# Summing squares over features: pairs of feature tiles added on GpSimd and VectorE ahead of one group of matmuls

## The chip, the cores and the metric

The kernel runs on one core of one Trainium2 chip. Its engines work side by side, each on its own queue in order: TensorE (matmul; PE in the profile, PEld for its weight loads), VectorE (DVE), ScalarE (ACT), GpSimd (POOL) and SyncE (SP, which issues most DMAs). The metric is the device time of one execution in microseconds. Before the change the median of three runs is 1806.03 us (1805.53 to 1806.41).

## What is computed

Two layers of a diffusion backbone run over 512 latent tokens and 256 context tokens, each a vector of 1024 features. What matters here is the sandwich norm around every mixer and every FFN:

```
def rms_norm(x, g):
    y = xf * lax.rsqrt(jnp.mean(xf * xf, axis=-1, keepdims=True) + EPS)
    return (y * g.astype(jnp.float32)).astype(x.dtype)

def modulate(h, shift, scale):
    return h * (1 + scale) + shift
```

A mixer or FFN gives y. The kernel computes x = x + gate * rms_norm(y), and then the next input h = modulate(rms_norm(x), shift, scale). So each token needs two sums of squares over its 1024 features: one of y, and one of the new x. Layer 0 mixes by neighbourhood attention and an mLSTM and carries both kinds of tokens; layer 1 mixes by latent attention and gives out latent tokens only. All arithmetic is float32, the large products as three products of split operands (hi and lo).

## The kernel before

Activations lie with features on the 128 partitions: eight feature tiles (KD = 8), each 128 features by a run of tokens. A run ("segment", class `Seg`) is all 512 latent tokens (`SX`), the 256 context tokens (`SC`), or one half of the latent tokens (`SH[0]`, `SH[1]`, 256 each).

The sum of squares over features runs across partitions, so TensorE makes it. `sums4` (line 390) takes four tiles of squares and multiplies each by a 128x32 matrix of ones; the four matmuls go to four column groups of the array (`tile_position`) and add into four bands of 32 partitions of one PSUM tile `ps`. Two calls, `first` and `last`, accumulate eight feature tiles. The matmul of the last tile is issued first and the other three are held behind it (`issue_after`). `sums_bc` (line 400) then copies the PSUM tile to a row (`scratch("srow")`), adds the four bands by small matmuls (`psc`), computes the inverse root (`rstd_of`: VectorE, one power instruction on GpSimd, three on VectorE) and broadcasts it over partitions by a transpose into PSUM (`bc`).

There are two places with such sums:

- `YNorm.put(m, src)` (line 420) is called once for each output tile m of an output projection or of the last down-projection group of an FFN. It squares the tile on ScalarE (`ysq`) and, after m = 3 and m = 7, calls `sums4` into `ysum`. (A 512-wide segment has another way: it adds its squares up on GpSimd in one tile, and is not touched.) The squares stand in two-tile buffers of the tag `sq`; there are two of these. The tag `sc` of `scratch` has two buffers of 128x512 as well.
- `YNorm.chain` (line 438) is a generator. Its first step makes the broadcast of y's norm; then for each k it scales y(k) on VectorE (line 453), adds it to x(k) on VectorE or, for the k of `RVO` = (1, 3) or `RVF` = (0, 2, 4), on GpSimd (line 454), squares x(k) into y(k) on ScalarE, and after k = 3 and k = 7 calls `sums4` into `pss`; then come the steps that make the modulated h. `RawNorm.chain` (line 482), for the last FFN part of layer 0, makes h from x(k) at once (lines 493 and 494) and applies the second norm later as a factor.

Chains are put in a list, and `step(n)` advances the oldest one by n steps while the next segment's projection is being traced: `out_proj` (line 1186) after each output tile, `ffn` (line 1219) in `front` and in `down`. So the chain of one segment runs beside the `put`s of the next one. Segments go in this order: out_proj of layer 0: SX, SC; FFN of layer 0: SH[1], SH[0], SC; out_proj of layer 1: SH[0], SH[1]; FFN of layer 1: SH[0], SH[1]. Of the nine `put` sequences eight use `sums4`; seven of the chains have a second norm. That makes 15 sums of 8 tiles, 30 calls of `sums4`.

The order of instructions on each engine isn't written by hand. The tile framework lays it from the order of tracing, priorities (`tc.high_priority` for weight loads) and its own idea of when operands are ready; waits and buffer releases are added by it.

The helpers in which the profile records the operations: `mm` L142, `tr` L145, `act` L148, `tt` L151, `ts` L154, `stt` L157, the matmul of `sums4` L393.

Of the kernel before, what the change touches and what calls it, by code (L numbers as in the profile page):

```python
# [9 lines left out]
F32 = mybir.dt.float32  # L10
F32R = mybir.dt.float32r
BF16 = mybir.dt.bfloat16
AF = mybir.ActivationFunctionType
ALU = mybir.AluOpType
# [3 lines left out]
KD = D // 128  # L18
# [46 lines left out]
def hybrid_backbone_kernel(ctx: ExitStack, tc: tile.TileContext, *aps):  # L65
    nc = tc.nc
    V, S, G, PE = nc.vector, nc.scalar, nc.gpsimd, nc.tensor
# [39 lines left out]
    def ps_c(name):  # L107
        if psum["split"]:
            psum["j"] = psum.get("j", 0) + 1
            return ps_t("yx"[psum["j"] % 2], name)  # L110
        return ps_t("c" if "c" in psum["n"] else "w", name)
# [26 lines left out]
    def instr(i):  # L138
        return getattr(i, "ins", i)

    def mm(o, l, r, start, stop):
        return PE.matmul(out=o, lhsT=l, rhs=r, start=start, stop=stop)  # L142
# [4 lines left out]
    def act(o, i, func=AF.Copy, **kw):  # L147
        S.activation(out=o, in_=i, func=func, **kw)  # L148

    def tt(e, o, x, y, op):  # L150
        e.tensor_tensor(out=o, in0=x, in1=y, op=op)  # L151

    def ts(e, o, x, s1, s2, op0, op1):
        e.tensor_scalar(out=o, in0=x, scalar1=s1, scalar2=s2, op0=op0, op1=op1)  # L154

    def stt(o, x, s, y, op0, op1):
        V.scalar_tensor_tensor(out=o, in0=x, scalar=s, in1=y, op0=op0, op1=op1)  # L157
# [6 lines left out]
    def fr(ap):  # L164
        return ap.bitcast(F32)
# [187 lines left out]
    sqp = ctx.enter_context(tc.tile_pool(name="sqp", bufs=2, reuse_waits="tile"))  # L353

    def scratch(name):
        return sqp.tile([128, 512], F32, tag="sc", name=name, bufs=2)

    def rstd_bc(pss, n, dim, name):

        return bcasts(rstd_of(pss[:, :n], n, dim), n, name)  # L360
# [29 lines left out]
    def sums4(ps, w, srcs, first, last):  # L390

        def one(i):
            return PE.matmul(out=ps[32 * i:32 * i + 32, 0:w], lhsT=ones32, rhs=srcs[i], start=first, stop=last,  # L393
                             tile_position=(0, 32 * i))
        n_ = len(srcs) - 1
        with tc.issue_after(instr(one(n_))):
            for i in range(n_):
                one(i)

    def sums_bc(ps, sg, name):  # L400

        row = scratch("srow")
        act(row[:, 0:sg.w], ps[:, 0:sg.w])
        psc = ps_c("psc")
        for j in range(sg.nt):
            mm(psc[:, j:j + 1], row[:, j * 128:(j + 1) * 128], sel4[:, 0:1], True, True)
        return rstd_bc(psc, sg.nt, D, name)

    class YNorm:


# [8 lines left out]
        def put(self, m, src):  # L420
            w = self.sg.w
            if self.wide:
                if m == 0:
                    act(self.acc, src, AF.Square)
                else:
                    sq = scratch("ysq")
                    act(sq[:, :w], src, AF.Square)
                    tt(G, self.acc, self.acc, sq[:, :w], ALU.add)
                return
            if m % 2 == 0:  # L430
                self.t = sqp.tile([128, 512], F32, tag="sq", name="ysq")
            sq = self.t[:, 256 * (m % 2):256 * (m % 2) + w]
            act(sq, src, AF.Square)
            self.sq.append(sq)
            if m % 4 == 3:
                sums4(self.ps, w, self.sq[-4:], m == 3, m == KD - 1)

        def chain(self, x, y, Gt, mod=None, done=None):


            sg = self.sg
            w, c = sg.w, sg.mc
            if self.wide:
                pss = ps_c("pssy")
                for j in range(sg.nt):
                    mm(pss[:, j:j + 1], self.acc[:, j * 128:(j + 1) * 128], ones_c, True, True)
                bc = rstd_bc(pss, sg.nt, D, "y")
            else:
                bc = sums_bc(self.ps, sg, "y")
            yield  # L450
            ps2 = ps_c("pss") if mod else None
            for k in range(KD):
                stt(y(k), y(k), Gt[:, k, c:c + 1], bc[:, :w], ALU.mult, ALU.mult)
                tt(G if k in (RVF if done and mod else RVO) else V, x(k), y(k), x(k), ALU.add)
                if mod:
                    act(y(k), x(k), AF.Square)
                    if k % 4 == 3:
                        sums4(ps2, w, [y(k - 3 + i) for i in range(4)], k == 3, k == KD - 1)
                else:
                    done(k)  # L460
                yield
            if mod:
                bc = sums_bc(ps2, sg, "m")
                yield
                A, B, h = mod
                for k in range(KD):
                    hi, lo = (t[:, k, sg.ho:sg.ho + w] for t in h)
                    b = B[:, k, c:c + 1]
                    stt(y(k), x(k), A[:, k, c:c + 1], bc[:, :w], ALU.mult, ALU.mult)
                    if k in (LGF if done else LGO):  # L470
                        ts(G, y(k), y(k), 1.0, b, ALU.mult, ALU.add)
                        act(hi, y(k))
                        tt(G, lo, y(k), fr(hi), ALU.subtract)
                    else:
                        act(hi, y(k), AF.Identity, bias=b)
                        stt(lo, y(k), b, fr(hi), ALU.add, ALU.subtract)
                    yield

    class RawNorm(YNorm):


        def chain(self, x, y, Gt, mod, done):
            sg = self.sg
            w, c = sg.w, sg.mc
            A, h = mod
            bc = sums_bc(self.ps, sg, "y")
            yield
            self.ps2 = ps_c("pss")
            for k in range(KD):
                stt(y(k), y(k), Gt[:, k, c:c + 1], bc[:, :w], ALU.mult, ALU.mult)  # L490
                tt(G if k in RVF else V, x(k), y(k), x(k), ALU.add)
                hi, lo = (t[:, k, sg.ho:sg.ho + w] for t in h)
                act(hi, x(k), AF.Copy, scale=A[:, k, c:c + 1])
                stt(lo, x(k), A[:, k, c:c + 1], fr(hi), ALU.mult, ALU.subtract)
                act(y(k), x(k), AF.Square)
                if k % 4 == 3:
                    sums4(self.ps2, w, [y(k - 3 + i) for i in range(4)], k == 3, k == KD - 1)
                yield

        def factor(self, y):  # L500
# [10 lines left out]
    with ExitStack() as l0:  # L511
# [20 lines left out]
        for k in range(KD):  # L532
            sq = x0p.tile([128, T], F32, tag="sq0", name="sq0", bufs=4)
# [168 lines left out]
        for i in range(7):  # L702
            src, dst = runs[i % 2], runs[1 - i % 2]
# [1093 lines left out]
```

## Time and profile before

| | |
|---|---|
| median of 3 runs | 1806.03 us |
| the profiled execution | 1806.48 us |
| its span, first to last instruction | 1804.3 us |
| mean granted TensorE clock | 0.991 |
| TensorE busy | 1739.2 us (96%), 10498 matmuls |
| VectorE busy | 1163.0 us (64%), 2210 instructions |
| ScalarE busy | 748.2 us (41%), 1297 |
| GpSimd busy | 253.7 us (14%), 306 |

The profile is of one execution. A row of the page gives an engine's busy time, its share of the span and its instructions. A row of a group names line, engine, operation, the tiles written and read, the shape, the count, then busy time and the mean in ns, then the idle time of the engine ahead of these instructions and what ended it. A row of a timeline gives start and duration in us from the span's start, and in square brackets the idle time just ahead with its releaser. `x8` means that eight records were merged into a row. A matmul's recorded duration overlaps the next one's, so the distance of starts tells what it costs. The tile name `acc` stands for y (line 1194 and line 1316), so a square of the new x in a chain is a ScalarE row `acc<-x`; `ysq` is a square in `put`, `ysum` and `pss` are the PSUM tiles of the two kinds of sums.

### The profile page before, as it was taken

The numbers are of one execution on the slowest core, as the hardware profiler recorded it, in microseconds if no ns is written. First come the engines' busy times: TensorE is split into PE (matmuls) and PEld (weight loads), VectorE is DVE, ScalarE is ACT, GpSimd is POOL, SyncE is SP. The second block draws the span as 40 slices with busy tenths as digits, with TensorE's granted clock in tenths as the row PEclk, the third lists the DMA queues.
The fourth block names the chain that finished last, engine by engine and source line by source line (L and its number), as shares of the span: only waits on it lengthen the run. The fifth ranks groups of instructions, "written<-read, shape, count | busy, mean of one in ns | idle before, by whom it ended". The sixth has DMA issues, their size and how long they took to land.

```text
span 1804.3 us, 26608 instructions
## 1 busy us (share of the span) xinstructions
PE 1739.2 (96%) x10498; PEld 1454.0 (81%) x10498; DVE 1163.0 (64%) x2210; ACT 748.2 (41%) x1297; POOL 253.7 (14%) x306
## 2 busy tenths in 40 slices
PE   6999999999999999999999999899999999999997
PEld 4777887887878888888888888788878888888885
DVE  3384577558266686676764657788894574556555
ACT  3333344444344422132221335577784454333242
POOL 1000024224320000000000002444451200000001
PEclk8999999999999999999999999999999999999998
DMA  9343332113312343444322211000012132224231
GB/s 307 106 139 129 95 112 88 53 54 127 96 36 94 120 130 108 137 127 132 120 87 70 82 47 48 24 12 13 13 36 85 50 115 87 89 86 135 72 94 47
DMA packets 63260, 162.39 MB, mean 90 GB/s; under 512 B 6272, under 2 KB 19792, under 8 KB 63136
## 3 DMA queue, kind: packets, MB, share of 16 engines
q1 hardware_dynamic: 61616, 156.52, 27.6%
q0 software_dynamic: 1376, 4.04, 0.7%
q8 instruction: 83, 1.36, 0.3%
q14 instruction: 41, 0.34, 0.1%
q10 hardware_dynamic: 144, 0.13, 0.0%
HBM read 158.57 MB, written 2.10 MB: 89 GB/s over the span
## 4 chain that ended last, share of the span: by engine, by line
PE 83%; DVE 7%; POOL 3%; issue 2%; DMA 2%; ACT 2%; DVEq 0%; POOLq 0%; ACTq 0%
PE pu L142 29%; PE pd L142 14%; PE sp L142 4%; PE qkp L142 3%; PE yps L142 3%; PE puf L142 3%; PE vtk L142 3%; PE pdl L142 3%; PE qp L142 2%; PE ot L142 2%; PE pt L145 2%; PE vp L142 2%; PE kp L142 2%; DMA aw<-in_ada_w_dram 1%; DVE acc L157 1%
## 5 line engine op out<-in xcount | busy, mean ns | idle before, releaser
L148 ACT ACTIVATE whi<-wraw 128x1024 fp32r<-128x1024 f32 x186 | 195.4, 1058 | 478.8 <-PE pu L142 221.1
L151 DVE TENSOR_TENSOR wlo<-wraw,whi 128x1024 fp32r<-128x1024 f32 x184 | 224.9, 1227 | 236.1 <-ACT whi L148 235.4
L142 PE MATMUL pu<-h,whi 128*128 128x258 f32 (+1 forms) x1280 | 318.5, 339 | 0.0
L142 PEld LDWEIGHTS pu<-h,whi 128*128 128x128 f32 x1280 | 219.6, 188 | 28.7 <-issue 0.8
L142 PE MATMUL pd<-hid,whi 128*128 128x512 f32 (+1 forms) x864 | 233.4, 358 | 1.5 <-DVE acc L151 1.5
L142 PE MATMUL pu<-h,wlo 128*128 128x512 f32 (+1 forms) x640 | 216.6, 339 | 0.0
L142 PEld LDWEIGHTS pd<-hid,whi 128*128 128x128 f32 x864 | 152.2, 188 | 28.6 <-DVE acc L151 3.1
L151 POOL TENSOR_TENSOR ry<-rv,mhalf 128x2 f32<-128x2 f32 (+2 forms) x26 | 24.1, 928 | 999.2 <-DVE rv L154 997.8
L142 PE MATMUL pd<-hid,wlo 128*128 128x512 f32 (+1 forms) x432 | 153.1, 356 | 0.0
L151 DVE TENSOR_TENSOR acc<-pd,acc 128x512 f32<-128x512 f32 (+1 forms) x192 | 109.2, 586 | 50.0 <-PE pd L142 48.7
L142 PEld LDWEIGHTS pu<-h,wlo 128*128 128x128 f32 x640 | 120.9, 189 | 13.7
L142 PE MATMUL pu<-hb,whi 128*128 128x512 f32 x304 | 119.5, 393 | 0.0
L142 PE MATMUL pu<-hb,wlo 128*128 128x512 f32 x304 | 119.3, 392 | 0.0
L142 PE MATMUL pu<-lb,whi 128*128 128x512 f32 x304 | 118.2, 389 | 0.0
L157 DVE SCALAR_TENSOR_TENSOR av<-aw,s,av 128x512 f32<-128x512 f32 x140 | 102.5, 749 | 18.9 <-DMA aw<-in_ada_w_dram 18.2
L154 POOL TENSOR_SCALAR P<-P,rl 128x768 f32<-128x768 f32 (+1 forms) x96 | 85.1, 889 | 140.4 <-DVE nm L154 49.1
L142 PEld LDWEIGHTS pd<-hid,wlo 128*128 128x128 f32 x432 | 81.2, 188 | 11.9
L157 DVE SCALAR_TENSOR_TENSOR u<-pu,c_ffn_conv,u 128x769 f32<-128x769 f32 x80 | 81.1, 1014 | 10.4 <-ACT u L148 9.7
L142 PE MATMUL sp<-kr,qh 128*128 128x512 f32 (+1 forms) x256 | 71.0, 353 | 2.5 <-ACT P L148 1.3
L151 DVE TENSOR_TENSOR pTl<-pt,pTh 128x512 fp32r<-128x512 f32 x96 | 64.5, 682 | 5.6 <-ACT pTh L148 4.8
L142 PEld LDWEIGHTS pu<-hb,wlo 128*128 128x128 f32 x304 | 57.1, 188 | 13.1
L142 PEld LDWEIGHTS pu<-lb,whi 128*128 128x128 f32 x304 | 57.1, 188 | 12.8
(454 smaller groups left out, 3799.9 us busy)
## 6 DMA issues: line engine op xcount, KB each, us to landing
wraw<-in_ffn_up_dram SPq DMA_DIRECT2D x88, 512.0 KB, 3.6
aw<-in_ada_w_dram SPq DMA_DIRECT2D x112, 256.0 KB, 2.8
wraw<-in_ffn_down_dram SPq DMA_DIRECT2D x44, 512.0 KB, 3.6
aw<-in_ada_w_dram SPq DMA_DIRECT2D x40, 512.0 KB, 4.6
wraw<-in_w_in_dram SPq DMA_DIRECT2D x20, 512.0 KB, 3.5
wraw<-in_w_tok_dram SPq DMA_DIRECT2D x8, 512.0 KB, 4.3
wraw<-in_w_out_dram SPq DMA_DIRECT2D x8, 512.0 KB, 3.6
wraw<-in_w_o_dram SPq DMA_DIRECT2D x8, 512.0 KB, 3.5
```

The lines of the kernel that those rows point to most:

```text
L142: return PE.matmul(out=o, lhsT=l, rhs=r, start=start, stop=stop)
L145: PE.transpose(out=o, in_=i, identity=ident[0:i.shape[0], 0:i.shape[0]])
L148: S.activation(out=o, in_=i, func=func, **kw)
L151: e.tensor_tensor(out=o, in0=x, in1=y, op=op)
L154: e.tensor_scalar(out=o, in0=x, scalar1=s1, scalar2=s2, op0=op0, op1=op1)
L157: V.scalar_tensor_tensor(out=o, in0=x, scalar=s, in1=y, op0=op0, op1=op1)
```

## The change

Squares of tiles k and k + 4 are added to each other before TensorE sums them. A new helper `pair` adds the square of tile k into the one of tile k - 4, in place: on GpSimd for k = 4, 5 and 6, on VectorE for k = 7. `sums4` is then called once for each run, with four tiles, first and last at once, after k = 7. In `put` the first four squares keep the two buffers of the tag `sq`, and the last four go to `scratch` tiles (`ysq2`). In both chains y(k) is added into y(k - 4). The wide way of `put` and the first norm of the kernel (line 536) are as they were.

```diff
+    def pair(sq, sq2, k):
+
+        tt(V if k == KD - 1 else G, sq, sq, sq2, ALU.add)
+
     class YNorm:
...
-            if m % 2 == 0:
-                self.t = sqp.tile([128, 512], F32, tag="sq", name="ysq")
-            sq = self.t[:, 256 * (m % 2):256 * (m % 2) + w]
-            act(sq, src, AF.Square)
-            self.sq.append(sq)
-            if m % 4 == 3:
-                sums4(self.ps, w, self.sq[-4:], m == 3, m == KD - 1)
+            if m < 4:
+                if m % 2 == 0:
+                    self.t = sqp.tile([128, 512], F32, tag="sq", name="ysq")
+                self.sq.append(self.t[:, 256 * (m % 2):256 * (m % 2) + w])
+                act(self.sq[m], src, AF.Square)
+            else:
+                if m % 2 == 0:
+                    self.t = scratch("ysq2")
+                sq = self.t[:, 256 * (m % 2):256 * (m % 2) + w]
+                act(sq, src, AF.Square)
+                pair(self.sq[m - 4], sq, m)
+            if m == KD - 1:
+                sums4(self.ps, w, self.sq, True, True)
...
                     act(y(k), x(k), AF.Square)
-                    if k % 4 == 3:
-                        sums4(ps2, w, [y(k - 3 + i) for i in range(4)], k == 3, k == KD - 1)
+                    if k >= 4:
+                        pair(y(k - 4), y(k), k)
+                    if k == KD - 1:
+                        sums4(ps2, w, [y(i) for i in range(4)], True, True)
...
                 act(y(k), x(k), AF.Square)
-                if k % 4 == 3:
-                    sums4(self.ps2, w, [y(k - 3 + i) for i in range(4)], k == 3, k == KD - 1)
+                if k >= 4:
+                    pair(y(k - 4), y(k), k)
+                if k == KD - 1:
+                    sums4(self.ps2, w, [y(i) for i in range(4)], True, True)
```

## The prediction

> **What bounds the kernel now.** I began with the page: the span, the busy times, and the chain that ended last.
>
> ```profile
> span 1804.3 us, 26608 instructions
> PE 1739.2 (96%) x10498; PEld 1454.0 (81%) x10498; DVE 1163.0 (64%) x2210; ACT 748.2 (41%) x1297; POOL 253.7 (14%) x306
> PE 83%; DVE 7%; POOL 3%; issue 2%; DMA 2%; ACT 2%; DVEq 0%; POOLq 0%; ACTq 0%
> ```
>
> TensorE is busy for 96% of the span and is 83% of the chain, so a matmul taken away is worth its time wherever TensorE has other work ready. GpSimd has 86% of the span free and VectorE 36%, but those are averages: the edit lies in four short stretches (about 450 to 540, 1060 to 1130, 1370 to 1430 and 1766 to 1793 us), and what counts is who is late there.
>
> Next I asked for the line of the summing matmuls (L393), on TensorE alone. The last two rows are TensorE's idle time ahead of them, with its releaser and the number of waits.
>
> ```profile
> L393 PE MATMUL ysum<-ysq,ones x128: 379/391/403, 499.0 to 1792.0; 128*32 128x256 f32 x128
> L393 PE MATMUL pss<-acc,ones x112: 379/403/617, 496.8 to 1428.6; 128*32 128x256 f32 x96, 128*32 128x512 f32 x16
>   ACT acc L148: 3.8, 5
>   ACT ysq L148: 2.8, 3
> ```
>
> There are 240 records. A group is four matmuls, and each float32 matmul leaves two records (a group shows as x8 below), so there are 30 groups: two for each of 15 runs of tokens, eight in `put` (ysum) and seven in the chains (pss). One pss run is 512 wide, all others 256. Half the groups go: 120 records.
>
> **What a group costs TensorE.** The third view is TensorE's timeline at the first two groups (start, duration).
>
> ```profile
> 496.39 0.28 PE L142 MATMUL yps<-h,wlo 128*128 128x256 f32 x1
> 496.51 0.28 PE L142 MATMUL yps<-h,whi 128*128 128x256 f32 x1
> 496.77 1.07 PE L393 MATMUL pss<-acc,ones 128*32 128x512 f32 x8
> 497.76 0.38 PE L142 MATMUL yps<-h,whi 128*128 128x256 f32 x1
> 497.99 0.28 PE L142 MATMUL yps<-h,wlo 128*128 128x256 f32 x1
> ...
> 498.69 0.28 PE L142 MATMUL yps<-h,wlo 128*128 128x256 f32 x1
> 498.81 0.28 PE L142 MATMUL yps<-h,whi 128*128 128x256 f32 x1
> 499.02 0.64 PE L393 MATMUL ysum<-ysq,ones 128*32 128x256 f32 x8
> 499.59 0.39 PE L142 MATMUL yps<-h,whi 128*128 128x256 f32 x1
> 499.81 0.29 PE L142 MATMUL yps<-h,wlo 128*128 128x256 f32 x1
> ```
>
> Ends overlap, so starts are what to read. Ordinary 256-wide matmuls start 0.12 us apart. Into the 256-wide group it is 0.21, from its start to the next matmul 0.57, and to the one after that 0.22: a group costs 0.09 + 0.57 + 0.10 = 0.76 us. The 512-wide one costs 0.14 + 0.99 + 0.11 = 1.24. Term one: 14 x 0.76 + 1.24 = 11.9 us less TensorE work.
>
> **What is added.** Each run gets three adds on GpSimd and one on VectorE: 45 and 15. These rows are groups of instructions: the nearest GpSimd adds (whole trace), and VectorE's in the last 50 us.
>
> ```profile
> L151 POOL TENSOR_TENSOR x<-acc,x 128x256 f32<-128x256 f32 x14 | 11.8, 840 | 21.2 <-DVE acc L157 21.2
> L151 POOL TENSOR_TENSOR ysq<-ysq 128x512 f32<-128x512 f32 x7 | 9.1, 1302 | 23.2 <-ACT ysq L148 23.2
> L151 DVE TENSOR_TENSOR x<-acc,x 128x256 f32<-128x256 f32 x12 | 4.8, 423 | 0.0
> ```
>
> So 0.84 us (512 wide: 1.30) per GpSimd add and 0.42 per VectorE add. [...]
>
> Together the GpSimd adds are about 39 us on an engine that is 14% busy. What counts is not their sum but when the last of them is done, for now one group waits for all eight squares, and whatever stands behind it on TensorE waits too.
>
> **The added step in `put`.** There the eight squares are paced by TensorE, one per output tile of about 1.4 us, so adds 4, 5 and 6 are done before square 7. Add 7 on VectorE comes between the last square and the group: 0.42 plus a hand-off of 0.04, 0.46 us. In six of the eight puts the next tile's or the next stage's matmuls are ready and can be laid ahead of the group; I cost these at nothing, and if that cover is missing it is 0.46 each, 2.8 in all. Two puts wait for their last square already, and there the step is exposed: 517.17 and the end of the kernel, 0.92 together. At the end the order is matmul, VectorE add, square, group, as these rows from the timelines show, among them groups I need below.
>
> ```profile
> 517.17 0.64 PE L393 MATMUL ysum<-ysq,ones 128*32 128x256 f32 x8 [1.06 <-ACT ysq L148]
> ...
> 1081.57 0.64 PE L393 MATMUL pss<-acc,ones 128*32 128x256 f32 x8 [0.68 <-ACT acc L148]
> ...
> 1086.62 0.40 ACT L148 ACTIVATE acc<-x 128x256 f32<-128x256 f32 x1
> 1086.75 0.48 DVE L157 SCALAR_TENSOR_TENSOR h<-x,A,h 128x256 fp32r<-128x256 f32 x1
> 1087.63 0.64 PE L393 MATMUL pss<-acc,ones 128*32 128x256 f32 x8
> ...
> 1790.81 0.42 DVE L151 TENSOR_TENSOR acc<-pdl,acc 128x256 f32<-128x256 f32 x1 [1.00 <-PE pdl L142]
> 1791.27 0.42 ACT L148 ACTIVATE ysq<-acc 128x256 f32<-128x256 f32 x1 [0.95 <-DVE acc L151]
> 1791.74 0.64 PE L393 MATMUL ysum<-ysq,ones 128*32 128x256 f32 x8 [0.97 <-ACT ysq L148]
> ```
>
> **The seven chains.** Here the squares hang on VectorE, not on TensorE. When the first group goes, so does its wait: of the 6.6 us of waits above, 1.06 and 0.97 are at last groups of puts, so 4.6 are at first groups. That isn't a gain by itself: TensorE reaches the one group earlier and waits there. Take the pair 1081.57 and 1087.63. Without the first group and its wait TensorE stands at the second at 1087.63 - 0.76 - 0.68 = 1086.19. Square 7 ends at 1087.02; VectorE is in another instruction until about 1087.2, adds, and hands over at about 1087.67. The wait is 1.48 where 0.68 was: +0.80. I take +0.80 for five of the 256-wide chains, 4.0 us. The sixth (chain of the context tokens in layer 0) gets 0: its last two squares, the first of the next rows, end at 527.18, and its second group starts seven microseconds later; other matmuls fill the time.
>
> ```profile
> 526.43 0.75 ACT L148 ACTIVATE acc<-x1c 128x256 f32<-128x256 f32 x2 [0.64 <-DVE x1c L151]
> ...
> 534.21 0.64 PE L393 MATMUL pss<-acc,ones 128*32 128x256 f32 x8
> ```
>
> The 512-wide chain is worse. Its squares and VectorE's residual adds:
>
> ```profile
> 496.08 1.67 ACT L148 ACTIVATE acc<-x 128x512 f32<-128x512 f32 x3
> 498.85 1.15 ACT L148 ACTIVATE acc<-x 128x512 f32<-128x512 f32 x2
> ...
> 497.42 1.29 DVE L151 TENSOR_TENSOR x<-acc,x 128x512 f32<-128x512 f32 x2
> ...
> 501.82 1.07 PE L393 MATMUL pss<-acc,ones 128*32 128x512 f32 x8
> ```
>
> And this is how a GpSimd add meets a VectorE instruction that reads two SBUF tensors:
>
> ```profile
> 1077.46 0.74 POOL L151 TENSOR_TENSOR x<-acc,x 128x256 f32<-128x256 f32 x1 [0.37 <-DVE acc L157]
> 1077.66 0.82 DVE L157 SCALAR_TENSOR_TENSOR h<-x,A,h 128x256 fp32r<-128x256 f32 x1 [0.28 <-ACT h L148]
> ...
> 1079.86 0.47 DVE L157 SCALAR_TENSOR_TENSOR h<-x,A,h 128x256 fp32r<-128x256 f32 x1
> ```
>
> The same instruction takes 0.47 us alone and 0.82 beside GpSimd, ending 0.28 after it: VectorE stood still for 0.35. So in the 512-wide chain add 4 (from 497.3 to 498.6) holds the sixth residual add up; they then take turns, VectorE to 499.25, GpSimd (add 5) to 500.55, VectorE to 501.2, GpSimd (add 6) to 502.5, VectorE (add 7) to 503.2. TensorE would stand there at 501.82 - 1.24 = 500.58 and wait 2.7 us. [...]
>
> Sum: -11.9 + 0.9 (two puts) + 4.0 (five chains) + 2.7 (the wide chain) = **-4.3 us**. Bounds: the last add could cost nothing anywhere (-11.9, and no better, since the first groups' waits are waits for the same squares), or 0.46 in the six covered puts too (-1.5).
>
> Nothing else is on the path. ACT issues the same squares, and no DMA moves. The two scratch buffers now also hold squares 4 to 7 of a `put` and are shared with the row copies of the sums; those come behind the last square. The squares 0 to 3 hold both buffers of their tag to the end of the put, where the next put wanted them anyway. VectorE's add 7 waits for ACT; behind it stand residual adds and PSUM additions of the next tile, which TensorE needs to get its PSUM banks back. Behind the adds that wait on GpSimd stand its residual adds and the power step of the next norm; since GpSimd is free for most of each stretch, I cost that at nothing, and if it is wrong at one add, 0.84, for the norm that it holds up.
>
> **Own time and median.** The profiled execution took 1806.48 us, 2.2 more than its span; the median of the runs is 1806.03. I take the sum off the median: 1806.0 - 4.3 = 1801.7 us.
>
> **Rivals.**
>
> (a) The order of instructions on each engine isn't written in the kernel; it will be laid anew, and if other matmuls fill every wait in the chains, only the two exposed puts pay: -11.9 + 0.9 = -11.0, 1795.0. For it: after most groups the next instruction is an unrelated matmul. Against: the five waits for ACT acc above, 3.8 us in all, show that the order fits the real squares only to about 0.8 us.
>
> (b) The gain is eaten. Each chain's three GpSimd adds hold VectorE up by 0.35 each, 1.05 per chain, in five chains 5.3 us if all hit and 2.6 if half do. -4.3 + 2.6 to -4.3 + 5.3 is -1.7 to +1.0: 1804.3 to 1807.0, no difference.
>
> (c) Slower: VectorE becomes the bound in the last down-projection of the first FFN. The view by stretches there:
>
> ```profile
> 1075.00:1088.00 13.00, 11.42 (x100) 9.64 (x100) 11.56 (x29) 8.37 (x22) 2.21 (x3) 1.00 0.00 0
> 1094.00:1107.00 13.00, 12.02 (x104) 10.05 (x103) 11.78 (x29) 9.49 (x24) 3.40 (x5) 1.00 0.02 4
> ```
>
> Columns after the length are TensorE, its weight loads, VectorE, ScalarE and GpSimd busy. VectorE has 1.2 to 1.4 us free of 13. In each stretch a chain and the next put run together: six GpSimd adds, 6 x 0.35 = 2.1, and add 7, 0.42, are 2.5 us. It decides from the point where more than half of the six hit a two-input instruction. Then on top of (b)'s 5.3 come the puts' adds, 2 x 1.05 here and 1.05 in the output projection of layer 1, and two adds 7 (0.84): -4.3 + 5.3 + 3.2 + 0.8 = +5.0, 1811.0. [...] Against it: about half of VectorE's instructions there read PSUM (the scaling by the broadcast, the additions of products) and run beside GpSimd, and between the stretches VectorE has room.
>
> That the change does nothing of what it says can be excluded: fewer matmuls are issued.
>
> **How the numbers follow.** About 0.2%, 3.6 us, is what a measurement of this kernel can tell from no change. Forecast 0.33, (a) 0.17, (b) 0.30, (c) 0.20. The forecast's middle is just over the line, so I count 0.02 of it as no difference: faster 0.48, same 0.32, slower 0.20. For the range I leave out the far half of (a) and most of (c): 1796.5 to 1809.5. Within faster and same alone it would be 1796.5 to 1807.
>
> **What would show it.** Right: 10378 matmuls on TensorE, 120 records at L393; TensorE's busy time 9 to 11 us lower; eight ysum and seven pss groups, with the pss groups waiting 1 to 3 us each and for an add on GpSimd or VectorE, no longer for ACT; 0.46 more at the end between the last square and the group. (a) would show TensorE's waits at L393 under 3 us in all. (b) and (c) would show two-input instructions of VectorE at 0.8 where they took 0.42 to 0.47, and (c) both stretches longer than 13 us. Wrong would be a gain or loss that comes from stages without these sums: then the new order of the instructions, not the sums, has decided.

## The result and the profile after

The change makes the kernel slower: 1824.55 us (median of 5 runs, 1823.20 to 1825.62) against 1806.23 us before on the same chip (1805.53 to 1806.93), a ratio of 1.0104 (95% interval 1.0091 to 1.0117). The forecast was 1801.7, the range ended at 1809.5. The profiled execution took 1825.62 us, its span is 19.4 us longer than before. Of all executions in this document one, of `e12` below, ran at a granted clock of 0.842 and took 1925.00 us; it is left out of the figures. The page after:

```profile
span 1823.7 us, 26435 instructions
PE 1743.6 (96%) x10378; PEld 1459.2 (80%) x10378; DVE 1174.1 (64%) x2225; ACT 748.3 (41%) x1297; POOL 297.6 (16%) x351
```

The 120 records are gone as said, yet TensorE is busy 4.4 us longer, not 9 to 11 us shorter: some of its work ran slower. With 19.4 us more span and 4.4 more busy it also stood still 15 us more. The view of TensorE's waits says for what (engine, tile, line, releaser; us in total, times, longest):

```profile
PE pdl L142 <- DVE acc L151: 8.2, 11, 2.2
PE ysum L393 <- DVE ysq L151: 6.2, 3, 4.5
PE puf L142 <- ACT whi L148: 2.6, 1, 2.6
PE pss L393 <- DVE acc L151: 1.2, 2, 1.1
PE pss L393 <- POOL acc L151: 0.8, 3, 0.4
```

At the groups themselves (the rows with L393) it is 8.2 us, against 6.6 before: the waits that the prediction had thought about hardly grew in sum, though one of them, 4.5 us, is new. The row at the top is another thing: products of the down-projection (`pdl`) that wait until VectorE has emptied their PSUM bank. Before it was

```profile
PE pdl L142 <- DVE acc L151: 1.7, 4, 0.6
```

Where the time went is read by stages. I cut each trace at the same three pairs of matmuls: the output projection of layer 0, the first FFN's last down-projection with what overlaps it, and the output projection of layer 1. The view by stretches of the kernel before (window, length, then busy us of TensorE, its weight loads, VectorE, ScalarE, GpSimd, the granted clock, DMA share, GB/s):

```profile
486.65:563.27 76.62, 73.14 (x492) 61.72 (x492) 54.30 (x103) 38.55 (x75) 16.70 (x16) 1.00 0.16 49
1039.85:1170.86 131.01, 119.79 (x890) 103.98 (x888) 91.26 (x222) 63.80 (x139) 30.98 (x37) 0.99 0.13 40
1364.10:1473.81 109.71, 104.61 (x778) 93.22 (x777) 64.34 (x117) 55.28 (x106) 15.67 (x17) 1.00 0.25 78
```

and of the kernel after:

```profile
488.09:573.47 85.38, 77.34 (x481) 64.54 (x481) 62.87 (x116) 39.76 (x78) 30.41 (x25) 0.96 0.18 56
1049.29:1187.48 138.19, 118.39 (x842) 103.18 (x841) 96.29 (x228) 64.06 (x139) 44.69 (x55) 0.99 0.12 38
1380.60:1493.63 113.03, 107.07 (x746) 96.58 (x745) 66.93 (x121) 55.58 (x106) 27.17 (x29) 0.95 0.25 75
```

The three stages grew by 8.8, 7.2 and 3.3 us, together 19.3 of the 19.4. Three different things are to be seen. In the first and third the granted clock fell: the trace's clock record has TensorE at half rate (a granted clock of 0.50) for 6.8 and 10.2 us there, where before had none, which costs half of it by estimate, 3.4 and 5.1. In the middle stage the clock is as before (3.4 us at half in both), TensorE's busy time fell by 1.4, and it stands still 19.8 us (138.19 - 118.39) instead of 11.2, while VectorE is busy 5.0 longer. And by the same estimate the third stage without its clock loss would have *gained* 1.8 us.

### The profile page after: what moved, and what is told of

The parts are those of the page before. It is cut to its first block, busy times and chain, and to the rows that moved or that the text cites. A ratio compares the mean times of both kernels' runs of the same rounds, so it can differ in the third digit from the quotient of the medians.

```text
span 1823.7 us, 26435 instructions
## 1 busy us (share of the span) xinstructions
PE 1743.6 (96%) x10378; PEld 1459.2 (80%) x10378; DVE 1174.1 (64%) x2225; ACT 748.3 (41%) x1297; POOL 297.6 (16%) x351
## 4 chain that ended last, share of the span: by engine, by line
PE 80%; DVE 9%; POOL 3%; ACT 2%; DMA 2%; issue 2%; DVEq 0%; ACTq 0%; POOLq 0%
PE pu L142 29%; PE pd L142 13%; PE puf L142 4%; PE sp L142 4%; PE qkp L142 3%; PE vtk L142 3%; PE yps L142 3%; PE qp L142 2%; PE pt L145 2%; PE ot L142 2%; PE vp L142 2%; PE kp L142 2%; PE pdl L142 2%; DVE wlo L151 1%; DVE acc L157 1%
## 5 line engine op out<-in xcount | busy, mean ns | idle before, releaser
L151 POOL TENSOR_TENSOR ysq<-ysq,ysq 128x256 f32<-128x256 f32 x24 | 19.7, 823 | 878.9 <-ACT ysq L148 878.9
L142 PEld LDWEIGHTS pd<-hid,wlo 128*128 128x128 f32 x432 | 81.2, 188 | 11.9
L142 PE MATMUL pdl<-hid,whi 128*128 128x256 f32 x320 | 61.1, 289 | 8.4 <-DVE acc L151 8.2
```

## The first stage in close-up

The 512-wide chain, on the timelines of GpSimd, VectorE and TensorE (the first row is three adds, the second is the first of them alone):

```profile
498.82 7.76 POOL L151 TENSOR_TENSOR acc<-acc 128x512 f32<-128x512 f32 x3 [2.55 <-ACT acc L148]
498.82 5.32 POOL L151 TENSOR_TENSOR acc<-acc 128x512 f32<-128x512 f32 x1 [2.55 <-ACT acc L148]
...
498.87 1.28 DVE L151 TENSOR_TENSOR x<-acc,x 128x512 f32<-128x512 f32 x2
500.07 1.22 DVE L151 TENSOR_TENSOR wlo<-wraw,whi 128x1024 fp32r<-128x1024 f32 x1
501.20 0.68 DVE L151 TENSOR_TENSOR acc<-acc 128x512 f32<-128x512 f32 x1
501.81 1.22 DVE L151 TENSOR_TENSOR wlo<-wraw,whi 128x1024 fp32r<-128x1024 f32 x1
...
502.71 1.04 PE L393 MATMUL pss<-acc,ones 128*32 128x512 f32 x2
504.19 1.04 PE L393 MATMUL pss<-acc,ones 128*32 128x512 f32 x2 [0.44 <-POOL acc L151]
505.41 1.04 PE L393 MATMUL pss<-acc,ones 128*32 128x512 f32 x2 [0.17 <-POOL acc L151]
506.63 1.05 PE L393 MATMUL pss<-acc,ones 128*32 128x512 f32 x2 [0.17 <-POOL acc L151]
507.61 0.51 PE L142 MATMUL yps<-h,whi 128*128 128x256 f32 x2
```

The first GpSimd add takes 5.32 us, the other two about 1.25 each. The prediction had the two engines take turns. Here they did not: VectorE goes through five instructions with two SBUF inputs without a pause, until 503.02, each at its usual length, and the GpSimd add ends 1.12 us after that. Two of the five are splits of weights, which stand at this place before the change too and which the prediction had not put into its turns. The four matmuls of the group, which before ran side by side in four column groups and took 0.99 us from their start to the next matmul, now start one by one as their squares arrive: 4.90 us from the first to the next matmul, most of it shown as *busy*. Then the `put` of the context tokens:

```profile
517.83 0.28 PE L142 MATMUL yps<-h,wlo 128*128 128x256 f32 x1
517.91 2.26 DVE L157 SCALAR_TENSOR_TENSOR h<-acc,mod,h 128x512 fp32r<-128x512 f32 x2
518.29 1.04 ACT L148 ACTIVATE whi<-wraw 128x1024 fp32r<-128x1024 f32 x1
519.50 0.37 ACT L148 ACTIVATE ysq<-yps 128x256 f32<-128x256 f32 x1
520.09 1.21 DVE L151 TENSOR_TENSOR wlo<-wraw,whi 128x1024 fp32r<-128x1024 f32 x1
520.47 1.78 POOL L151 TENSOR_TENSOR h<-acc,h 128x512 fp32r<-128x512 f32 x1 [0.84 <-ACT h L148]
521.23 1.31 DVE L151 TENSOR_TENSOR ysq<-ysq,ysq 128x256 f32<-128x256 f32 x1
522.59 0.86 PE L393 MATMUL ysum<-ysq,ones 128*32 128x256 f32 x8 [4.48 <-DVE ysq L151]
523.38 1.22 PE L142 MATMUL puf<-h,whi 128*128 128x512 f32 x2
```

The last square is done at 519.87. VectorE is then in the chain's `h` and the weight split until 521.30, and the add itself takes 1.31 us beside a GpSimd add that lasts until 522.25; in `e1` below, with no GpSimd add beside it, it takes 0.41. TensorE's queue has the group right behind the last product of the projection, so it stands still for 4.48 us, not 1.06 + 0.46. Before, eight matmuls of the next stage (`puf`) lay between the two:

```profile
513.98 0.28 PE L142 MATMUL yps<-h,wlo 128*128 128x256 f32 x1
514.09 0.63 PE L142 MATMUL puf<-h,whi 128*128 128x512 f32 x2
...
515.49 0.63 PE L142 MATMUL puf<-h,whi 128*128 128x512 f32 x2
517.17 0.64 PE L393 MATMUL ysum<-ysq,ones 128*32 128x256 f32 x8 [1.06 <-ACT ysq L148]
```

So of the 3.4 us by which the wait grew, 1.9 are work that no longer lies ahead of the group (514.26 to 516.12). The other 1.6 are the later group: 1.4 of VectorE's queue and 1.3 of add, less 1.1 because ScalarE's last square now comes 1.8 us after the last product and not 2.9. The `puf` pair after the group takes 1.22 us, where a pair at full clock takes 0.63 (515.49 above): half clock.

## The experiments

After the result I held these theories. **W**: the one group waits for the adds on GpSimd and VectorE, chiefly in the chains, and the clock falls after these standstills. **L**: VectorE and GpSimd have no room for the adds; the adds alone cost it. **O**: the new order of instructions has TensorE reach a group with nothing laid ahead of it. **C**, beside these: what is lost is half clock behind standstills, wherever they are. **B** came later: the shared scratch buffers couple `put` and chain. Every ratio is to the kernel before on the same chip.

| | median us | before | ratio (95%) |
|---|---|---|---|
| `e1_put_only` | 1816.34 | 1805.85 | 1.0053 (1.0038 to 1.0068) |
| `e2_chains_only` | 1807.66 | 1805.85 | 1.0008 (0.9999 to 1.0018) |
| `e3_all_vector` | 1819.75 | 1805.85 | 1.0070 (1.0054 to 1.0087) |
| `e4_no_adds` | 1802.68 | 1805.85 | 0.9978 (0.9967 to 0.9988) |
| `e5_adds_only` | 1812.24 | 1806.24 | 1.0032 (1.0022 to 1.0043) |
| `e7_filled` | 1827.25 | 1806.24 | 1.0110 (1.0093 to 1.0127) |
| `e8_filler` | 1823.82 | 1806.24 | 1.0089 (1.0073 to 1.0105) |
| `e9_not_ffn0` | 1817.24 | 1806.24 | 1.0051 (1.0035 to 1.0068) |
| `e10_own_buffers` | 1824.39 | 1806.50 | 1.0098 (1.0083 to 1.0113) |
| `e11_layer1_chains` | 1804.86 | 1806.50 | 0.9990 (0.9981 to 0.9999) |
| `e12_layer0_as_before` | 1811.73 | 1806.50 | 1.0027 (1.0015 to 1.0040) |
| `e13_layer1_all` | 1808.55 | 1806.50 | 1.0014 (1.0003 to 1.0025) |

**Which half.** `e1_put_only` takes the change in `put` alone; `e2_chains_only` the other way round. Against the changed kernel, `e1`:

```diff
-                    if k >= 4:
-                        pair(y(k - 4), y(k), k)
-                    if k == KD - 1:
-                        sums4(ps2, w, [y(i) for i in range(4)], True, True)
+                    if k % 4 == 3:
+                        sums4(ps2, w, [y(k - 3 + i) for i in range(4)], k == 3, k == KD - 1)
```

(the same in `RawNorm`), and in `e2` the lines of `put` as before.

> Pairs in the eight puts alone; the seven chains sum in two groups as before. Theory W (the one group waits for adds that GpSimd and VectorE hold back from each other, chiefly in the chains, TensorE then stands and its granted clock halves): the change took 18.3 us more than before, nearly all of it from the chains' side, so this comes out between 4 us faster and 1 us slower than before, with no new stretch at half clock. Rival L (every added add costs VectorE time in the full stretches of the first FFN's end, whoever waits): about 3 to 4 us slower than before, from those stretches. Rival O (only the new order of instructions decides): anything, with the loss in places that have no sum.

> Pairs in the seven chains alone; the puts sum in two groups as before. Theory W: 12 to 19 us slower than before, with the 512-wide chain's group stretched over about 5 us on TensorE again and at least one new stretch at half clock. Rival L: half of the adds, so about half of the loss, 8 to 10 us. Rival O: anything.

The puts alone cost 10.5 us, the chains alone 1.8, not certainly anything. That refutes W's place: the loss isn't chiefly the chains'. The first stage says the same: 76.6 us before, 78.2 in `e2`, 84.3 in `e1`, 85.4 with the whole change. The two halves make 12.3 of the 18.3, the rest comes only from both together. In the trace of `e1` the context `put` of layer 0 is the worst single wait:

```profile
519.99 1.08 PE L393 MATMUL ysum<-ysq,ones 128*32 128x256 f32 x8 [5.13 <-DVE ysq L151]
521.00 1.22 PE L142 MATMUL puf<-h,whi 128*128 128x512 f32 x2
```

**The adds and the groups apart.** `e3_all_vector` gives all adds to VectorE. `e4_no_adds` sums only the last four squares of each run, with no adds: half of the squares are left out of the sums. `e5_adds_only` is the kernel before with all adds made into tiles that nobody reads any more.

```diff
 e3
-        tt(V if k == KD - 1 else G, sq, sq, sq2, ALU.add)
+        tt(V, sq, sq, sq2, ALU.add)
 e4, in put; the same in the chains
-            if m % 4 == 3:
-                sums4(self.ps, w, self.sq[-4:], m == 3, m == KD - 1)
+            if m == KD - 1:
+                sums4(self.ps, w, self.sq[-4:], True, True)
 e5, against the kernel before
+                    if k >= 4:
+                        pair(y(k - 4), y(k - 4), y(k), k)
                     if k % 4 == 3:
```

> All four adds of each run on VectorE, none on GpSimd. Theory W (what is late is GpSimd's add and its turns with VectorE): 12 us or more of the 18.3 come back, so at most 6 us slower than before, and the 512-wide group costs about 1 us of TensorE again. Rival L (VectorE has no room): 60 adds of 0.42 us on VectorE, eight of them in each of the two full stretches, 3.4 us each: as slow as the change or slower, 18 us or more over before.

> Leaves work out: the squares of tiles 4 to 7 alone are summed in one group, nothing is added, so the norms see half of the features. It shows what the 15 groups are worth on TensorE alone. Theories W and L: 8 to 12 us faster than before (11.9 by the prediction's term one, less some waits that move to the one group). Rival O: the new order costs by itself, so it is less than 5 us faster, or slower.

> The kernel before, both groups kept, and the change's 60 adds made beside them for nothing (in the chains into tiles that the first group has read, in the puts into the scratch tiles). No sum waits for an add. Theory L (the two full stretches of VectorE in the first FFN's end have no room for the adds): the part from the end of the plain down-projections to the attention (before: 1040 to 1171) grows by 5 to 9 us, as with the change. Rival W (it is the sums that wait for adds): that part grows by less than 2 us. Layer 0's output projection grows by less than 4 us under both, since the group stands where it stood in TensorE's order.

The 15 groups are worth 3.2 us even where nothing is added, not 11.9, which is what O expected of `e4` (less than 5). The adds alone cost 6.0. All on VectorE the change loses 13.9 instead of 18.3, between what W (at most 6) and L (18 or more) expected. The stretches of `e4` say where the 11.9 stay:

```profile
487.53:567.14 79.61, 74.15 (x481) 64.22 (x481) 59.07 (x113) 39.47 (x78) 16.89 (x16) 0.96 0.19 60
1042.95:1172.90 129.95, 115.89 (x841) 101.73 (x840) 91.08 (x222) 64.13 (x139) 31.55 (x37) 1.00 0.13 41
1366.00:1471.90 105.90, 101.80 (x746) 93.01 (x745) 64.40 (x117) 55.71 (x106) 15.68 (x17) 1.00 0.25 80
```

Layer 1 gives its four groups in full (109.71 to 105.90, 3.8 for 3.0). In the middle stage TensorE's busy time falls by 3.9 (six groups, 4.6 by the prediction's price) and its idle time rises by 2.8 (14.06 against 11.22): it gets to VectorE's PSUM additions sooner and waits there. In layer 0 the context `put`'s group stands right behind the last product, as with the whole change and as in `e1`, without the eight matmuls that lay between them before; it waits 3.15 us for ScalarE's last square, and the clock falls (0.96). Where a `put` keeps its two groups (`e2`, `e5`) the eight are still there. So it is merging the groups of a `put`, and not the adds, that moves the group ahead of them; why the framework lays it so, these runs don't show.

**The context put of layer 0.** `e7_filled` holds its group back behind matmuls that are traced later; `e8_filler` lays twenty matmuls of 128x512 ahead of it, work that is of no use.

```diff
 e7
+                if sg is SC:
+                    yield
+                    with tc.issue_after(instr(mms[-12])):
+                        sums4(self.ps, w, self.sq, True, True)
                 bc = sums_bc(self.ps, sg, "y")
 e8
             if m == KD - 1:
+                if self.sg is SC and not isinstance(self, RawNorm):
+                    for i in range(20):
+                        mm(self.ps[:, 512:1024], h[0][:, 0, 0:128], h[0][:, 1, 0:512], True, True)
                 sums4(self.ps, w, self.sq, True, True)
```

> The change, with one group moved in TensorE's order: the sum of the context tokens' y in layer 0 is issued behind 18 matmuls of the next stage, as it was behind 9 or more before. Theory O (TensorE reached that group with nothing laid ahead of it, stood 4.5 us and lost 3.4 more to the half clock): layer 0's output projection, 8.8 us longer with the change, is 1 to 4 us longer than before, no half clock near 520, and the whole 4 to 8 us below the change. Rival (the late add itself holds the chain of the context tokens up, and with it the next stage): the wait turns up again within 30 us and the whole stays within 2 us of the change.

> The change, with 20 useless matmuls of 512 columns (about 4.4 us of TensorE) laid ahead of that same group, into a free half of its PSUM tile. They do no work; they only keep TensorE busy while it would stand. If standing still is what halves the clock, there is no half clock near 520 and the whole is 2 to 3.5 us below the change, with more work done. If the clock halves for another reason, the time is that of the change or up to 4 us more.

Both miss. In `e7` that group no longer waits, but the 512-wide chain's now stands still for 3.04 us, and half clock follows it. The first FFN's stage, which `e7` doesn't touch, has 13.7 us of half clock instead of 3.4 and takes 140.5 us instead of 138.2, so the clock hides part of what the move is worth. In `e8` the wait and the half clock behind it are gone, as was expected if standing still halves the clock, but not the 2 to 3.5 us: the twenty matmuls take 4.83 us themselves, and 3.4 us of half clock stand at 513.9 instead, behind a wait of 1.42. O is right that nothing is laid ahead; no run lays useful work there and leaves all else in place, so what the order alone costs is not measured.

**The first FFN.** `e9_not_ffn0` leaves the first FFN as before and changes the rest. `e10_own_buffers` is the change with one two-tile buffer of their own for squares 4 to 7 there, where the change has two shared ones.

```diff
 e9, in put (and RawNorm's chain as before)
+            if isinstance(self, RawNorm):
...
+                if m % 4 == 3:
+                    sums4(self.ps, w, self.sq[-4:], m == 3, m == KD - 1)
+                return
 e10
-                    self.t = scratch("ysq2")
+                    if isinstance(self, RawNorm):
+                        self.t = self.pool.tile([128, 512], F32, name="ysq2", tag="ysq", bufs=1)
+                    else:
+                        self.t = scratch("ysq2")
```

> The change everywhere but in the end of the first FFN, where all six sums stay in two groups. Theory L: the 7.2 us that this part was longer go, and the whole is 6 to 8 us below the change, 10 to 12 over before. Rival W or O: the loss there was one of order or clock and turns up elsewhere; the whole is within 3 us of the change.

> The change, but in the last down-projection of the first FFN the squares of tiles 4 to 7 of a put lie in a buffer of their own instead of the two scratch buffers that the row copies of the sums use too. Theory B (shared buffers): with the shared buffers ScalarE's order has square 6 of the put behind the chain's row copy, which waits for the chain's one group; with its own buffer square 6 stands ahead of it, so put and chain no longer wait for each other. It expects square 6 less than 1 us after its VectorE addition (2.6 us with the change) and the 7.2 us by which this stage had grown to fall under 3: about 1819 to 1821, ratio 1.007 to 1.0085. Theory L (VectorE has no room there for the adds and for the turns with GpSimd): the stage keeps 5 to 7 us, 1823 to 1825.

`e9` is 7.3 us faster than the change, as L expected, and its stage is again as long as before; the loss doesn't turn up elsewhere, as W and O expected:

```profile
1046.10:1177.15 131.05, 119.53 (x890) 103.82 (x889) 90.99 (x222) 64.01 (x139) 31.06 (x37) 0.99 0.13 41
```

What coupling there was is seen on ScalarE's queue. With the change the squares 6 and 7 of a `put` stand behind the row copy of the chain's sum, 2.3 us after the addition that makes tile 6 (VectorE, 1095.64 to 1096.05):

```profile
1095.64 0.41 DVE L151 TENSOR_TENSOR acc<-pdl,acc 128x256 f32<-128x256 f32 x1
...
1098.08 0.39 ACT L148 ACTIVATE srow<-pss 128x256 f32<-128x256 f32 x1 [1.51 <-PE pss L393]
1098.36 0.71 ACT L148 ACTIVATE ysq<-acc 128x256 f32<-128x256 f32 x2
```

In `e10` they stand ahead of it:

```profile
1096.06 0.40 ACT L148 ACTIVATE ysq<-acc 128x256 f32<-128x256 f32 x1
1097.07 0.42 ACT L148 ACTIVATE ysq<-acc 128x256 f32<-128x256 f32 x1 [0.61 <-DVE acc L151]
1097.61 0.39 ACT L148 ACTIVATE srow<-pss 128x256 f32<-128x256 f32 x1
```

From this segment's broadcast (`bcy`) to the next one's it is then 19.1 us instead of 21.6 (18.4 before); but the segment after it takes 24.5 instead of 24.0, the stage shrinks by 1.5 us only (138.19 to 136.65), and the medians can't be told apart. B has the coupling right and its price wrong: under 3 left was expected, 5.6 are, which is what L expected of this run.

**What is left of it.** `e11_layer1_chains` has the pairs in the two chains of layer 1 alone, `e13_layer1_all` in all of layer 1, `e12_layer0_as_before` everywhere except in layer 0's output projection and in the context tokens' `put` of the first FFN, with `e10`'s buffer. (The condition `self.sg is SC` holds for that `put` too, so eleven groups are merged and not the twelve that its expectation counts.)

```diff
 e11, e12, e13, in the chains
+                    if sg is SX or sg is SC:
+                        if k % 4 == 3:
+                            sums4(ps2, w, [y(k - 3 + i) for i in range(4)], k == 3, k == KD - 1)
+                    else:
...
 e12, in put; e13 the same for RawNorm too, and RawNorm's chain as before
+            if self.sg is SC:
...
+                return
```

> The kernel before, with pairs in the two chains of layer 1's output projection alone (two groups fewer, six adds on GpSimd and two on VectorE). By the prediction's price, 0.80 of wait against 0.76 of group each, nothing: 1806. By the stage of the chains-alone run (layer 1 was 1.3 shorter and the end 1.0): 1804 to 1805, ratio 0.999 to 1.000. If TensorE stands still 2 us or more at one of the groups, half clock adds 1.7 to 3.4: 1807 to 1809.

> The change with its own buffer in the first FFN as in the run beside it, and with the put of the context tokens and the two chains of layer 0's output projection as before (24 adds and 12 groups of the change remain less those: 12 groups are still merged). Theory B: layer 0's output projection gives back its 8.8 us and the FFN stage all but 3 of its 7.2, layer 1 keeps up to 3.3: 1808 to 1812, ratio 1.001 to 1.003. Theory L: FFN stage keeps 5 to 7: 1813 to 1817.

> The kernel before, with pairs only in layer 1: two chains and two puts of the output projection and two puts of the second FFN, six groups fewer. By groups alone -4.6 us, by the run without any add in this stage -3.9 and -1.4 at the end, so with room for the adds 1802 to 1804. If TensorE, there sooner, waits for the split of the next weights and the clock halves as with the change (its layer 1 was 3.3 longer, half clock 10.2 us): 1807 to 1809.

`e11` is 1.6 us faster than before, less than the 0.2% that I had called tellable, and its interval ends just below 1 (0.9999): the best of these runs that sums every square, but hardly told from no change. `e13`, with four more groups gone, is 2.0 us slower than before, its interval just above 1. Its trace shows where: TensorE is done with the projection 2.4 us sooner (last product at 1409.74, before at 1412.13) and waits for the next weights, whose split stands on ScalarE behind the chain's last steps (1410.58 to 1412.57).

```profile
1412.62 0.38 PE L142 MATMUL puf<-hb,whi 128*128 128x256 f32 x1 [2.60 <-ACT whi L148]
1414.07 0.58 PE L142 MATMUL puf<-hb,wlo 128*128 128x256 f32 x1 [0.95 <-DVE wlo L151]
```

6.8 us at half clock follow; with the whole change the same two waits stand at 1430.32 and 1431.77 and 10.2 us follow. Before, ScalarE's two splits at this place end later still (1413.75), but 23 `puf` matmuls ran without a wait from 1412.25 on, ahead of the `put`'s group, the first of them before either split was done; in `e13` and with the change five lie there. So here too the order was laid anew. `e12` was expected at 1808 to 1812 by B and at 1813 to 1817 by L. At 1811.73 (1808.76 to 1814.52) it lies at the edge of B's range and decides little. Its edit is `e13`'s with five of the six sums of the first FFN merged in addition, which makes these worth 3.2 us by the medians on one chip, where the stage in `e10`'s trace grew by 5.6 for six.

The middle stage of all of them, less half of the time at half clock (1.7 us for 3.4 of it). The idle time is length less TensorE's busy time and keeps all clock. In `e13`, whose code in this stage is that of before, the stage took 130.2 us with no half clock, where the second column has 129.3 for before: so that column is good to about 0.9 us.

| kernel | stage us | less clock | TensorE idle | VectorE busy |
|---|---|---|---|---|
| before | 131.0 | 129.3 | 11.2 | 91.3 |
| `e9_not_ffn0` | 131.05 | 129.3 | 11.5 | 91.0 |
| `e4_no_adds` | 129.95 | 129.95 | 14.1 | 91.1 |
| `e5_adds_only` | 132.8 | 131.1 | 11.85 | 96.6 |
| `e2_chains_only` | 132.4 | 132.4 | 13.7 | 95.85 |
| `e1_put_only` | 132.4 | 132.4 | 14.3 | 91.7 |
| `e10_own_buffers` | 136.65 | 134.95 | 18.1 | 96.1 |
| after | 138.2 | 136.5 | 19.8 | 96.3 |
| `e3_all_vector` | 141.0 | 137.6 | 21.6 | 98.2 |

Groups merged without adds: +0.6. Adds without merging: +1.8 (W expected under 2 of `e5` here, L 5 to 9). Both: +7.2. So neither the lost room on VectorE (L) nor the missing groups (O) carries it alone, but what joins them. The traces suggest how: the one group waits for adds that stand in line on VectorE and GpSimd, the norm and the next chain start later, and TensorE's products wait for VectorE's PSUM additions that stand in that chain (the `pdl` row, 8.2 us). 1.5 of it was the shared buffers; `e5` uses these too, so its 1.8 may hold some of the 1.5. How the other 3.3 (7.2 - 0.6 - 1.8 - 1.5) divide between the two queues isn't settled by these runs.

## Why the prediction was wrong

By the stages the 19.4 us of the profiled execution are: clock 8.5 (3.4 and 5.1, the estimate above), the middle stage 7.2, the first stage without its clock 5.4, the third without its clock -1.8, all else +0.1. The steps one by one:

- **Term one, -11.9.** The size of a group was right, where TensorE goes on: 3.8 us for four groups in layer 1 and 1.5 at the end for two (`e4`). The step that failed is to count it in every stage. In the first FFN VectorE sets the pace (in `e4` TensorE's idle time there rose by 2.8 as its busy time fell by 3.9), in layer 0 ScalarE's last square does, once nothing lies ahead of the group (a wait of 3.15); a group that goes there only moves the wait.
- **The two exposed puts, 0.92.** At the end it is exact: the group waits 1.43 us where it waited 0.97, and the releaser is VectorE's `ysq`. At 517 the 0.46 turned into 3.4 (4.48 against 1.06). The add was priced alone, 0.42 us on an idle VectorE: it met 1.4 us of queue and took 1.31. And the order was taken to stay: 1.9 us of the next stage's matmuls, which ran ahead of the group, now come behind it.

```profile
1811.15 0.64 PE L393 MATMUL ysum<-ysq,ones 128*32 128x256 f32 x8 [1.43 <-DVE ysq L151]
```

- **"In six of the eight puts the next tile's or the next stage's matmuls are ready ... I cost these at nothing."** The largest failure: the puts alone are +10.5. Matmuls of the next stage were laid behind the group instead (23 became five in layer 1), and the matmuls beside it wait for VectorE's PSUM additions or for split weights, so they were no cover.
- **The chains, +4.0, and the 512-wide one, +2.7.** With their groups (-0.76 x 6 - 1.24 = -5.8) the prediction makes `e2` +0.9 (4.0 + 2.7 - 5.8); measured +1.8, interval -0.2 to +3.3. Right in sum, partly by luck: in `e2`'s trace the middle stage is 1.4 us longer and the third 1.3 shorter, where these terms give about 0.1 each. In the wide chain the turns came as predicted in `e2` (three adds in 4.69 us, then a wait of 2.18). With the whole change they didn't come: the adds end at 506.6 and not 503.2, and the group costs 3.9 more than before (4.90 - 0.99), not 2.7.
- **"The two scratch buffers ... come behind the last square."** Wrong: the chain's row copy stands between the squares of the next `put`. It is 1.5 us in the trace, nothing that the medians show.
- **"Nothing else is on the path."** The clock was. The text never asked whether TensorE's granted clock would fall after a standstill, as it did here after 4.48 and 2.60 us, though the page shows the clock for every slice.
- **Three of four adds on GpSimd.** With all four on VectorE, `e3` is 4.4 below the change (13.9 against 18.3 over before), but 2.8 longer in the middle stage.
- **Rival (a)**, other matmuls fill every wait, is refuted: nothing was laid ahead at 517. **Rival (b)**, the gain is eaten, went the right way and was too small (at most 1807.0). **Rival (c)** named the right stage and engine, and its sign held: VectorE's residual adds beside GpSimd went from 0.41 to 0.69 us on average. These are the groups of instructions of VectorE in the first FFN's last part, before (1075 to 1113) and after (1084 to 1130):

```profile
L151 DVE TENSOR_TENSOR x<-acc,x 128x256 f32<-128x256 f32 x10 | 4.1, 413 | 0.0
```

```profile
L151 DVE TENSOR_TENSOR x<-acc,x 128x256 f32<-128x256 f32 x10 | 6.9, 686 | 0.0
```

  That is 2.7 us, and the four adds 7 there are another 2.1; but the `h` rows (`h<-x,A,h`, 16 of them) fell from 9.0 to 8.0 us in the same windows, so some 3.8 are left of its 2.5 for each of two stretches. Its size failed since it let TensorE lose only what VectorE lost: VectorE's 5.0 more cost TensorE 7.2, and alone (`e5`) 1.8.
- **The signs.** Right: 10378 matmuls, 120 records at L393, 0.46 at the end, VectorE's residual adds longer (its `h` rows were not). Wrong: TensorE's busy time (+4.4), and the pss groups, which wait 2.0 us in all and not 1 to 3 each.

## What to carry to other kernels

Removing work from the busiest engine paid here in the stage in which that engine didn't wait for another one right behind (`e4`: 3.8 us for four groups in layer 1), and not where it did (+0.6 for six in the first FFN); look at what its next instruction waits for, stage by stage, before the saved work is counted. A step that is put between a producer and a group of matmuls is priced with its engine's queue at that moment, not with its duration alone: the add of 0.42 us met 1.4 of queue and took 1.31. A small edit can also move a group ahead of the matmuls that covered its wait, as happened here twice, so cover is to be read from the trace after the change. And behind standstills of TensorE half clock came on top here, 3.4 us of it after 1.94 (`e5`) and 10.2 after 2.60 and 0.95 (the change).

## What the hardware showed

**The clock.** Half rate came in pieces of 3.4 us, or several of them in a row. In each trace all of them start on one grid of 3.41 us (with the change at 522.88, 1168.00 and 1430.82: 189 and 77 steps of 3.413 apart). Each stretch of that grid between 400 and 1780 us of the 13 traces (without `e12`), if it was at full clock itself, tells this: of those in which TensorE was busy for less than 44.5% half clock followed all 16, from there to 75% it followed 17 of 152, above 75% none of 5034. In the traces of before and after alone it is 2 of 2, 2 of 26 and none of 771. The length of a standstill alone didn't settle it: one of 2.19 us in the first FFN brought none with the change and 3.4 us in `e7`. In layer 0 standstills of 5.13 us (`e1`), 4.48 (after), 4.51 (`e9`), 3.15 (`e4`) and, in `e7`, 3.04 were followed by 6.8 us, 2.18 (`e2`) and 1.94 (`e5`) by 3.4. Of the 23 waits of 0.8 to 1.6 us that stand by themselves between 400 and 1780 us of before and after, one (0.90 at 1054.74, before) was followed by 3.4. The 2.60 and 0.95 in layer 1, 1.4 us apart, brought 6.8 (`e13`) or 10.2 (after), 1.26 and 0.95 in `e1` brought 6.8. `e11` has 3.4 at 486.7, in a stage that it doesn't touch, behind a wait of 0.89: so a single piece proves little.

**GpSimd beside VectorE.** Where a GpSimd add met VectorE instructions that read two SBUF tensors, it was VectorE that stood at some places and GpSimd at another. In the first FFN VectorE's adds of 0.41 us took up to 0.97 with the change; its additions of products from PSUM (`acc<-pdl,acc`) took 0.41 to 0.43 there both beside a GpSimd instruction (11) and without one (13). In the wide chain of `e2` the two went by turns (adds that take 0.68 us on VectorE and 1.25 on GpSimd took up to 1.8). With the change a GpSimd add took 5.32 us while VectorE went on at full pace. What decides between these isn't shown here.

**Column groups.** Four matmuls in four column groups ran side by side where their operands were there together, 0.99 us for the 512-wide group before, and one by one with the change, 4.90 us as the squares came.
